# Rebuilding the output projections and MLPs of a two-layer trunk as one stream of matmul groups

## The chip, the cores and the metric

The kernel runs on all 8 cores of one Trainium2 chip, one batch element a core; no core exchanges data with another. A core has TensorE (PE, matmuls), VectorE (DVE), ScalarE (ACT), GpSimd (Pool) and SyncE (SP), and 16 DMA engines, as the page of the profile counts them. The metric is the device time of the slowest core in microseconds, as the median of all executions.

Executions of one kernel fall in two states. In the slow one the four cores of a die (0 to 3 or 4 to 7), or of both, are granted a lower TensorE clock for part of the run. An execution is called slow when one die is over 1% longer than the other at a lower clock, or when it is over 1.5% above the fastest of its kernel. Kernels are compared fast against fast.

## The reference, cut to what matters

```python
# x: (8, 2048, 2048) f32. One mLSTM layer, then one latent-attention layer.
for layer in range(2):
    if layer == 0: mix = mlstm_mixer(x, ...)            # ends in  (sigmoid(o) * hn) @ w_out
    else:          k, v = shared_latent_kv(x, ...);  mix = mla_mixer(x, k, v, ...)   # ends in  o @ w_out
    x = layer_norm(DN_ALPHA * x + mix, ln1_g[layer], ln1_b[layer])
    x = layer_norm(DN_ALPHA * x + square(relu(x @ w1)) @ w2, ln2_g[layer], ln2_b[layer])
```

D is 2048 and D_FF 8192. Each core has 2048 tokens. For a core, one output projection is 1024 matmuls of 128x128 by 128x512, one MLP is 8192.

## The kernel before

It runs its stages one after the other: mLSTM, output projection, MLP, K/V/Q projections, attention, output projection, MLP. A barrier of all engines and all DMAs ends each. A helper records every operation with the buffers that it reads and writes and puts in the semaphore waits; each engine's own operations stand in its program in the order in which they were recorded, and the traces show them in it.

```python
# mLSTM: the convolution weights come with channels on the partitions, four bytes at a time
for j in range(4):
    ld(cw.t[:, :, j], conv_w[j].rearrange("(c p) -> p c", p=128), cw.b[0], allow_slow_non_contiguous=True)
ld(cw.t[:, :, 4], conv_b.rearrange("(c p) -> p c", p=128), cw.b[0], allow_slow_non_contiguous=True)
ld(nwb.t[:], norm_w.partition_broadcast(128), nwb.b[0])
# [...]
def phase_out(C, a_d, aB, fm, W, x_res, xresB, g, b, x_out, xoutB):
    # [... buffers; the whole weight is loaded here, after the barrier ...]
    for nt in range(4):
        P.dma("pool", lambda e, nt=nt: e.dma_start(out=wres[:, :, nt * 512:(nt + 1) * 512],
              in_=W[:, nt * 512:(nt + 1) * 512].rearrange("(k p) n -> p k n", p=128)), writes=[wresB[nt]])
    # [...] prep(tt): load 512 rows of the residual and of a; transpose a on PE
    prep(0)
    for tt in range(S // 512):
        # [...]
        if tt + 1 < S // 512:
            prep(tt + 1)
        stage_tm(...)                        # 16 groups of 16 matmuls, evacuated by DVE
        layernorm_tiles_act(...)             # four norms: three passes on ACT, two on Pool each, and small operations; then x_out to DRAM
    P.barrier()

def phase_mlp2(C, x_in, w1, w2, g, b, x_out, xinB, xoutB):
    # [...]
    build_xT(0)                              # x from DRAM, f32, transposed on PE
    for stile in range(S // 1024):           # two halves of 1024 tokens
        # [... load the eight residual tiles ...]
        for q in range(4):
            # [...] 32 groups h = x @ w1; ACT evacuates with Relu, then Square
            if q == 3 and stile + 1 < S // 1024:
                build_xT(stile + 1)
            # [...] 32 groups xs += h @ w2; DVE evacuates
        layernorm_tiles(C, [xs[:, sub, :] for sub in range(NS)], xsb, gb, bb, gbB, st, store)
    P.barrier()

def layernorm_stats(C, z, zb, stset):        # DVE: 4 bn_stats, 1 bn_aggr; ACT: Ln, Exp; DVE: 1
def layernorm_apply(...):                    # ACT: one pass (scale, bias); DVE: * g, then + b
def layernorm_tiles(...):                    # all eight stats, then all eight apply + store
```

The softmax here doesn't subtract the row's maximum and nothing guards it: scores larger than these inputs give would overflow.

## Time and profile before

| | before |
|---|---|
| recorded first: 6 executions | 7166, 7172, 7191 us (fast), 7402, 7622, 7692 us (slow); median 7296.87 |
| profiled execution (fast), slowest core | 7183.2 us |
| PE busy | 6038.4 us, 84% |
| start to start of two 128x512 matmuls in the MLPs | 0.216 us, clock 1.00 |

From the page: the span, busy time with share of the span and instructions, PE's busy tenths and the granted PE clock in 40 equal slices, and the chain of waits by engine.

```profile
span 7183.2 us, 78102 instructions; the slowest of 8 cores (7125.8 to 7183.2 us)
...
PE 6038.4 (84%) x28080; PEld 2729.0 (38%) x28080; DVE 1675.8 (23%) x2766; ACT 1683.1 (23%) x2829; POOL 811.8 (11%) x1099
...
PE   5899944589999789998488699968499999699995
...
PEclk9999966889999899999799899989799999899997
...
PE 78%; DMA 8%; ACT 4%; POOL 4%; DVE 3%; issue 3%; another core or an unknown queue 1%; SPq 1%; ACTq 0%; DVEq 0%; POOLq 0%
```

PE is nearly always busy inside a stage and falls to 4 tenths at the borders. That is where time can be had: 1145 us of the span are without a matmul. The waits of PE say for what (who, for whom, us in total, times, longest):

```profile
PE p L1290 <- DMA t<-x: 239.7, 18, 84.5
PE p L906 <- DMA t<-hg_d: 206.5, 7, 73.3
PE p L495 <- DMA t<-x: 95.8, 10, 87.0
PE p L427 <- DMA t<-oT_d: 80.0, 2, 61.9
PE p L1312 <- ACT t L1315: 75.8, 2, 38.1
PE p L1312 <- DMA t<-mlp_w: 56.8, 2, 33.0
PE p L671 <- DVE xT_43 L677: 45.9, 3, 43.3
...
PE p L1136 <- DMA t<-v_d: 18.0, 1, 18.0
```

L906 is the transposes of the first output projection, L1290 those of the MLP's x, L427 the projections' matmuls, L1312 the MLP's first matmuls, L1136 attention. The releaser named is the last to come. A wait for x at L1290 is at bottom a wait for the norms before it: x is stored, passes the barrier and is loaded again.

Busy time by stretch (from:to, length, then busy us and instructions of each engine, granted clock, DMA share, GB/s). The rows are the first output projection; the inside of an MLP; the border between the MLP's halves; the first MLP's tail; the last tail.

```profile
902.80:1362.80 460.00, 248.82 (x1281) 123.68 (x1280) 56.14 (x87) 103.94 (x111) 126.20 (x96) 0.76 0.39 106
...
1700.00:2270.00 570.00, 570.00 (x2642) 258.42 (x2641) 48.41 (x70) 116.48 (x190) 22.83 (x20) 1.00 0.50 76
2440.00:2560.00 120.00, 56.23 (x242) 24.59 (x243) 46.12 (x37) 39.54 (x53) 2.28 (x2) 0.72 0.67 175
3378.30:3466.00 87.70, 0.68 (x4) 0.71 (x5) 61.62 (x65) 19.86 (x24) 0.00 (x0) 0.52 0.29 116
...
7102.00:7183.20 81.20, 0.23 (x2) 0.00 (x0) 61.61 (x65) 19.86 (x24) 0.00 (x0) 0.52 0.25 104
```

At the start, the SP queue's own timeline shows the load of the convolution weights (start, length, queue, line, what, count). Its pieces hold the queue from 2.9 to 37 us, and the norm weight behind them comes late. VectorE waits 59 us for that weight, and PE waits 43 us for VectorE. The pieces have 4 bytes, and a load of 8 KB made of them took 24.6 us to land (median of four).

```profile
2.91 26.48 SPq L588 DMA_DIRECT2D cw_105<-a_conv_w  x4
29.43 7.51 SPq L588 DMA_DIRECT2D cw_105<-a_conv_b  x1
36.99 10.10 SPq L588 DMA_DIRECT2D nwb_106<-a_norm_w  x1
```

### The profile page before, as it was taken

How to read it: one execution, taken by the hardware profiler on the slowest of the kernel's cores; microseconds unless marked ns; L12 is line 12 of the kernel's file. 1: busy time of each engine (PE TensorE's matmuls, PEld its weight loads, DVE VectorE, ACT ScalarE, POOL GpSimd, SP SyncE). 2: the span in 40 equal slices, each digit the busy share in tenths (PEclk: the TensorE clock that was granted, in tenths of full speed). 3: DMA queues.
4: the chain of work that ended last, by engine and by line, in shares of the span. 5: the costliest groups of instructions: out<-in, count | busy, mean ns of one | idle time of the engine just before them, and what ended most of it. 6: DMA issues, size and time to landing. Idle time of an engine off the chain costs nothing.

```text
span 7183.2 us, 78102 instructions; the slowest of 8 cores (7125.8 to 7183.2 us)
## 1 busy us (share of the span) xinstructions
PE 6038.4 (84%) x28080; PEld 2729.0 (38%) x28080; DVE 1675.8 (23%) x2766; ACT 1683.1 (23%) x2829; POOL 811.8 (11%) x1099
## 2 busy tenths in 40 slices
PE   5899944589999789998488699968499999699995
PEld 3444422244444334443233222213244444244442
DVE  2566610101110400012332333321100111311004
ACT  2233321221112212210222144432322112211221
POOL 1111122400000000000022400004400000000000
PEclk9999966889999899999799899989799999899997
DMA  6433163275454555452564411135454545545452
GB/s 80 49 44 48 25 148 100 67 161 78 75 78 94 116 97 81 73 80 47 167 109 86 76 60 57 58 91 149 138 139 72 81 73 100 145 71 80 73 81 72
DMA packets 591304, 631.36 MB, mean 88 GB/s; under 512 B 187472, under 2 KB 556496, under 8 KB 566992
## 3 DMA queue, kind: packets, MB, share of 16 engines
q0 software_dynamic: 418320, 332.48, 32.5%
q1 hardware_dynamic: 172608, 293.89, 12.2%
q8 instruction: 233, 3.82, 0.2%
q14 instruction: 143, 1.17, 0.1%
HBM read 845.01 MB, written 113.77 MB: 133 GB/s over the span
## 4 chain that ended last, share of the span: by engine, by line
PE 78%; DMA 8%; ACT 4%; POOL 4%; DVE 3%; issue 3%; another core or an unknown queue 1%; SPq 1%; ACTq 0%; DVEq 0%; POOLq 0%
PE p L1328 25%; PE p L1312 24%; PE p L713 6%; PE p L427 5%; PE p L530 3%; PE p L684 3%; PE p L1147 2%; DMA t<-x 2%; PE p L1138 2%; PE p L1136 2%; PE p L1149 2%; POOL t L361 1%; POOL t L362 1%; DVE t L323 1%; DMA t<-hg_d 1%
## 5 line engine op out<-in xcount | busy, mean ns | idle before, releaser
L1312 PE MATMUL p<-t 128*128 128x512 bf16 x8192 | 1780.4, 380 | 136.1 <-ACT t L1315 75.8
L1328 PE MATMUL p<-t 128*128 128x512 bf16 x8192 | 1770.7, 379 | 0.0
L1312 PEld LDWEIGHTS p<-t 128*128 128x128 bf16 x8192 | 803.4, 98 | 1110.4 <-issue 150.6
L1328 PEld LDWEIGHTS p<-t 128*128 128x128 bf16 x8192 | 801.6, 98 | 966.1
L1315 ACT ACTIVATE t<-p 128x512 f32<-128x512 f32 x512 | 305.6, 597 | 2467.2 <-PE p L1312 2467.2
L1335 DVE TENSOR_TENSOR t<-p,t 128x512 f32<-128x512 f32 x384 | 265.6, 692 | 2163.3 <-PE p L1328 2163.3
L391 POOL DMA_DIRECT2D t<-mlp_w x128 | 146.3, 1143 | 3663.8 <-PE p L1312 1935.7
L427 PE MATMUL p<-t 128*128 128x512 bf16 x2048 | 449.7, 383 | 85.2 <-DMA t<-oT_d 80.0
L1141 ACT ACTIVATE t<-p 128x512 bf16<-128x512 f32 (+3 forms) x640 | 340.2, 533 | 500.8 <-PE p L1138 498.8
L530 PE MATMUL p<-t 128*128 128x512 bf16 x1408 | 325.1, 394 | 79.9 <-DMA t<-b_w_uq 36.3
L1316 ACT ACTIVATE t<-t 128x512 bf16<-128x512 f32 x512 | 322.1, 629 | 48.3 <-ACT t L1315 1.5
L427 PEld LDWEIGHTS p<-t 128*128 128x128 bf16 x2048 | 201.6, 99 | 331.7 <-issue 95.3
L1155 DVE RECIPROCAL t<-p 128x512 f32<-128x512 f32 x64 | 214.9, 3358 | 468.2 <-PE p L1149 459.5
L1290 PE MATMUL p<-ident_sb,t 128*128 128x128 f32 x512 | 93.1, 360 | 241.1 <-DMA t<-x 239.7
L1147 PE MATMUL p<-t 128*128 128x512 bf16 (+3 forms) x640 | 238.1, 372 | 48.8 <-POOL t L1143 38.3
L1332 DVE SCALAR_TENSOR_TENSOR t<-t,p 128x512 f32<-128x512 f32 x128 | 88.0, 688 | 794.2 <-PE p L1328 794.2
L1136 PE MATMUL p<-t 128*128 128x512 bf16 (+3 forms) x640 | 237.0, 370 | 22.6 <-DMA t<-v_d 18.0
L713 PE MATMUL p<-wvo_112,xT_43 128*128 128x512 bf16 x1024 | 233.6, 382 | 22.0 <-DMA wvo_112<-a_w_in 22.0
L530 PEld LDWEIGHTS p<-t 128*128 128x128 bf16 x1408 | 140.0, 101 | 265.3 <-issue 117.0
L1138 PE MATMUL p<-t 64*128 64x512 bf16 (+3 forms) x640 | 238.3, 372 | 0.0
L1149 PE MATMUL p<-t 128*128 128x512 bf16 (+3 forms) x640 | 236.4, 369 | 0.0
L713 PE MATMUL p<-wvo_46,xT_43 128*128 128x512 bf16 x1024 | 231.1, 379 | 0.0
(361 smaller groups left out, 4080.7 us busy)
## 6 DMA issues: line engine op xcount, KB each, us to landing
t<-mlp_w POOLq DMA_DIRECT2D x128, 2048.0 KB, 15.2
t<-x SPq DMA_DIRECT2D x112, 1024.0 KB, 14.4
x<-t SPq DMA_DIRECT2D x48, 1024.0 KB, 3.8
out<-t SPq DMA_DIRECT2D x16, 1024.0 KB, 3.8
wvo_46<-a_w_in POOLq DMA_DIRECT2D x8, 1024.0 KB, 20.4
wvo_112<-a_w_in POOLq DMA_DIRECT2D x8, 1024.0 KB, 18.3
t<-a_w_out POOLq DMA_DIRECT2D x4, 2048.0 KB, 78.5
t<-hg_d SPq DMA_DIRECT2D x16, 512.0 KB, 20.5
```

What stands on the lines that cost most here:

```text
L427: e.matmul(out=pbanks[sub][:], lhsT=lhsT_fn(kc, sub), rhs=rhs_fn(fc), start=first, stop=last),
L530: e.matmul(out=bank[0:m, :], lhsT=wt[:, kc * width + fc * 128: kc * width + fc * 128 + m], rhs=xT[:, kc, tokt * 512:(tokt + 1) * 512], sta ...
L713: P.op("pe", lambda e, kc=kc: e.matmul(out=bk[:], lhsT=xT.t[:, kc, tile * 128:(tile + 1) * 128], rhs=wt[:, kc, :], start=(kc == 0), stop=( ...
L1136: P.op("pe", lambda e, i=i, kt=kt, q0=q0, n=n, ps_=ps_: e.matmul(out=ps_[:, 0:n], lhsT=kn[i][:, kt * 128:(kt + 1) * 128], rhs=qn[i][:, q0: ...
L1138: P.op("pe", lambda e, i=i, kt=kt, q0=q0, n=n, ps_=ps_, r0=r0: e.matmul(out=ps_[:, 0:n], lhsT=kr[r0:r0 + 64, kt * 128:(kt + 1) * 128], rhs ...
L1141: P.op("act", lambda e, pt=pt, ps_=ps_, n=n: e.activation(out=pt[:, 0:n], in_=ps_[:, 0:n], func=AF.Exp, scale=SCALE), reads=[psB], writes= ...
L1147: P.op("pe", lambda e: e.matmul(out=po[:, c0:c0 + n], lhsT=vv[i][:, kt, :], rhs=pt[:, 0:n], start=(kt == 0), stop=(kt == nk - 1)), reads=[ ...
L1149: P.op("pe", lambda e: e.matmul(out=pm[:, c0:c0 + n], lhsT=onesb[:], rhs=pt[:, 0:n], start=(kt == 0), stop=(kt == nk - 1)), reads=[oB, ptB ...
L1312: e.matmul(out=bank[:], lhsT=wt[:, kc * 512 + fc * 128: kc * 512 + (fc + 1) * 128], rhs=xT[:, kc, tk * 512:(tk + 1) * 512], start=(kc == 0 ...
L1315: P.op("act", lambda e, r=r, bank=bank: e.activation(out=r[:], in_=bank[:], func=AF.Relu), reads=[bankB], writes=[rB])
L1316: P.op("act", lambda e, r=r, f=f, tk=tk: e.activation(out=hT[:, f, tk * 512:(tk + 1) * 512], in_=r[:], func=AF.Square), reads=[rB], writes ...
L1328: e.matmul(out=bank[:], lhsT=hT[:, fc, sub * 128:(sub + 1) * 128], rhs=wt[:, fc * 512:(fc + 1) * 512], start=(fc == 0), stop=(fc == 15)),
```

## The change

Intent: keep PE fed across the borders. Work that is not a matmul group is cut in pieces, and each piece is recorded a set number of groups ("slots") after the one that makes its input. Norms leave ACT: statistics and both passes are on DVE, one small power is on Pool. In layer one the projection's weight and first residual and rows are loaded during mLSTM's last head. In layer two the weight is loaded during attention, the rows and the residual after the barrier that ends attention and stays. The first MLP half takes the second 1024 tokens, whose transposed bf16 x the projection leaves on chip; the first 1024 go to DRAM and are read back for the second half. The barriers between mLSTM, projection and MLP go. The convolution weights come as two row loads and a PE transpose; the second v/o weight is loaded a token tile earlier. The input x now comes as f32 over the SP queue and is cast on VectorE and ScalarE (before, Pool's queue loaded it as bf16), and mLSTM's pieces are spaced anew. The core of the diff:

```diff
+class Slots:
+    def later(self, k, fn): # run fn when k more groups have been recorded
+    def slot(self):         # one more group: run what is due
 # mLSTM start
-    for j in range(4):
-        ld(cw.t[:, :, j], conv_w[j].rearrange("(c p) -> p c", p=128), cw.b[0], allow_slow_non_contiguous=True)
+    ld(cwr.t[0:64, :], conv_w.rearrange("j (c p) -> (j c) p", p=128), cwr.b[0])
+    P.op("pe", lambda e: e.transpose(out=pb[3][:, 0:80], in_=cwr.t[:], identity=C.ident[0:80, 0:80]), ...)
 # norms: [...] all of layernorm_stats / _apply / _tiles / _tiles_act goes
+def ln_rstd(C, st, stB):
+    P.op("dve", lambda e: e.bn_aggr(out=st[:, 24:26], in_=st[:, 0:24]), ...)
+    P.op("dve", lambda e: e.tensor_scalar(out=st[:, 26:27], in0=st[:, 25:26], scalar1=LN_EPS, ..., op0=ALU.add), ...)
+    P.op("pool", lambda e: e.tensor_tensor(out=st[:, 27:28], in0=st[:, 26:27], in1=C.mhalf[:], op=ALU.pow), ...)
+def ln_apply(C, st, stB, z, zB, gT, bT):  # two DVE passes of 2048 columns: (z - mean) * g, then * rstd + b
 # output projection [...]
+    def finish(self, sub, gT, bT):
+        ln_rstd(C, st, stB)
+        def apply():
+            ln_apply(C, st, stB, z[:], zB, gT, bT)
+            zb, zbB = self.zb.next()
+            P.op("act", lambda e: e.activation(out=zb[:], in_=z[:], func=AF.Copy), ...)   # bf16
+            # [...] rows 0 to 1023 are also stored
+            def trans():
+                transpose_sub(C, self.tb, zb, zbB, xT.t[:, :, ...], xT.b[0])
+                if sub == 3 or sub == 7:
+                    P.dma("sp", lambda e: e.dma_start(out=self.xT_d[i // 4], in_=xT.t[:]), ...)
+            C.S.later(3, trans)
+        C.S.later(1, apply)
+    def run(self, banks, gT, bT, ring_ready, done=None):
+        for sub in range(14):
+            for nt in range(4):
+                self.group(sub, nt, banks)        # 16 matmuls, DVE evacuates and takes statistics
+                # [...] load(sub + 2), prep(sub + 1)
+                S_.slot()
+            S_.later(1, lambda sub=sub: self.finish(sub, gT, bT))
+        for nt in range(4):
+            for sub in (14, 15):
+                self.group(sub, nt, banks)
+                S_.slot()
+            self.w[nt].free()
+            ring_ready(nt)                        # an MLP panel buffer there; its load one slot later
 # MLP [...]: three panel buffers instead of two, hT in four tiles
+                    w2_group(w, q, nt, sub)
+                    if q == 3 and nt == 3:
+                        S_.later(1, lambda half=half, sub=sub, s=st[sub]: finish(half, sub, *s))
+                S_.later(2, pan.load)
 # whole program
-            phase_mlstm(...)
-            C.P.barrier()
-        phase_out(...)
-        phase_mlp2(...)
+            fin = phase_mlstm(..., freed)          # freed(): loads of the projection as mLSTM's buffers go
+            out_and_mlp(op, 0, banks, gT, bT, fin, x1B, x1TB, x2, x2B)
+            P.barrier()
         phase_kvq(...)
+        for nt in range(4):
+            op.load_w(nt, top=True)                # second weight, under attention
         phase_att(...)
```

## The prediction

> **What bounds it now.** TensorE, except where a stage ends. The page gives PE 84% busy; the chain of waits is 78% PE. In the MLPs 128x512 matmuls start 0.216 us apart at granted clock 1.00 (timeline, stretches), so those stages are at their floor: 8192 matmuls a layer, about 1775 us. [...] What is left is TensorE idle time between stages. From its timeline: start to first projection 72 us, 62 idle; second v/o weight 22; end of mLSTM to first MLP matmul 594, 321 idle; first MLP 1881, 86 idle; norm tail, barrier, reload 87; attention to second MLP's first matmul 443, 189 idle; second MLP 1870, 78 idle; last norm 81.
>
> **What changes.**
> - Start: the convolution weights came by four-byte pieces, which held the SP queue some 35 us and blocked the norm weight, hence VectorE. Now two row loads and a transpose. First projection near 40-45 us, limited by weight transfers: -28 us.
> - Second v/o weight loaded a token tile earlier: -20.
> - First output projection: weights (which landed 41 to 96 us after issue), residual and rows are there before mLSTM ends. Norms no longer form a serial ScalarE/Pool tail (gaps of 73, 70, 84 us); x goes to the MLP through bf16 transposes among matmul groups. Estimate: 1024 x 0.216 + 512 transposes x about 0.07 = 260, with remnants 270. 594 to 270: -324.
> - MLPs: no f32 transposes (L1290, 93 us busy in all), no wait for a half's eight norms (38+33, 38+24 us): 1881 to 1785 and 1870 to 1785: -181.
> - Tails: a norm is about 1.4 us statistics and two passes of 2.3 us (0.692 us per 512 columns, 2.29 per 2048), against 3.5 us of PE per group, so VectorE falls about 25 us behind over the last eight groups. End tail about 32 us, the one before K/V about 40: -96.
> - Second output projection: weights load under attention; after the barrier one row tile and one residual tile: about 15 us instead of 62, then 221 + 23. 443 to 270: -173.
> - Given back: 16 MB of f32 weights compete with attention's first heads: +10.
>
> Unchanged: mLSTM's body (6 us idle in 673), K/V/Q (147 idle), attention (53).
>
> The sum is -812; from 7183 about 6370, all on TensorE's chain. VectorE does about 11 us per 17 us row block in the projections, so does not become the bound.
>
> **Prediction: 6370 us (8 in 10: 6270 to 6520).** The upper side allows for the slow state, which half the executions before show. Faster by over 2%: 0.98; within 2%: 0.015; slower: 0.005.
>
> **What will show it.** PE 92-94% busy. Output projection plus MLP about 2055 us in each layer. No PE gap over 10 us between the mLSTM's last matmul and the first MLP's last. Matmul spacing still 0.216 us. Mean granted clock about 0.97: [...] (0.5 after each long gap). DVE busy time changes little; ACT loses about 250 us.
>
> **What would make it wrong.** [...] buffers handed over late, so that panels or residuals start late; VectorE behind, holding PSUM banks at half boundaries; transfers in the first output projection (about 2.5 MB per 17 us) slower than needed; the first MLP panels landing late.

The floor of 1775 us a layer is the estimate from 8192 matmuls at the 0.216 us of the trace (1769). The clock of 0.5 is read from the clock records of the trace before: in the stretch of the first MLP's tail they show 0.5 from 3381.5 to 3470.2 us, where PE is idle from 3378.3 to 3465.3. The gap from 21 to 65 us, at the start, lies ahead of the first record.

## The result, and the profile after

Ratios are the mean time of one kernel's fast executions over that of the other's in the same rounds, so they are not quite the ratio of the medians.

| | before | after |
|---|---|---|
| all executions, median | 7391.78 us (20) | 6664.97 us (10) |
| range | 7161.89 to 7783.56 | 6401.07 to 7041.99 |
| fast executions | 8 of 20, 7162 to 7246 | 3 of 10: 6401, 6412, 6420 |
| profiled execution (fast) | 7183.2 us | 6396.1 us |
| fast over fast | | 0.8921 (95%: 0.8874 to 0.8969) |

The fast executions lie 30 to 50 us above the forecast of 6370. The recorded median lies 145 us above the upper end of its range, because 7 of the 10 executions were slow. These are two different findings, and the rest keeps them apart.

The same lines of the page after:

```profile
span 6396.1 us, 77157 instructions; the slowest of 8 cores (6334.3 to 6396.1 us)
...
PE 5962.3 (93%) x28081; PEld 2663.5 (42%) x28081; DVE 1874.9 (29%) x2958; ACT 1511.6 (24%) x2589; POOL 524.2 (8%) x937
...
PE   6999999999999999995887599989999999999997
...
PEclk8999999999999999997998799999999999999998
...
PE 84%; DMA 6%; DVE 4%; issue 2%; ACT 2%; POOL 1%; SPq 0%; another core or an unknown queue 0%; ACTq 0%; DVEq 0%; POOLq 0%
```

PE's busy time fell by 76 us, its idle time from 1145 to 434 us (span less busy): nine tenths of the gain is idle time. PE's waits after; L999 is the MLP's first matmuls, L884 the projections, L1284 attention, L426 the K/V/Q stage:

```profile
PE p L1284 <- DMA t<-v_d: 52.0, 1, 52.0
PE p L426 <- DMA t<-x: 48.3, 6, 45.6
...
PE p L999 <- DMA wp_143<-mlp_w: 22.1, 2, 11.8
...
PE p L999 <- DMA wp_184<-mlp_w: 15.8, 2, 9.4
PE p L884 <- DMA aT_165<-oT_d: 15.7, 1, 15.7
...
```

Three of the biggest waits of before (240, 207 and 80 us) have shrunk to one of 16. One has grown: attention's wait for its first head, from 18 to 52 us. Small ones are new, for the MLP's weight panels (wp). By stretch: the whole first projection; the inside of an MLP; after the border of the halves; both tails.

```profile
858.50:1112.60 254.10, 249.90 (x1509) 128.28 (x1510) 165.31 (x219) 85.27 (x77) 16.78 (x24) 1.00 0.51 158
1200.00:2000.00 800.00, 800.00 (x3708) 362.66 (x3707) 104.97 (x153) 133.40 (x218) 33.65 (x30) 1.00 0.52 82
...
2070.00:2130.00 60.00, 48.30 (x211) 21.32 (x212) 0.00 (x0) 16.20 (x27) 2.28 (x2) 0.89 1.01 197
2913.50:2959.20 45.70, 0.06 (x2) 0.06 (x1) 31.14 (x27) 0.00 (x0) 2.74 (x5) 0.54 0.42 169
...
6355.00:6396.00 41.00, 0.00 (x0) 0.00 (x0) 31.04 (x27) 0.00 (x0) 2.74 (x5) 0.53 0.37 154
```

The start, on the SP queue: the convolution weights now take two short issues, and x follows at 4.58 us.

```profile
2.91 0.56 SPq L520 DMA_DIRECT2D cwr_114<-a_conv_w  x1
3.51 0.56 SPq L520 DMA_DIRECT2D cwr_114<-a_conv_b  x1
```

The table below, worked out from the traces, sets the forecast against the result. A stretch runs from a stage's first matmul to the next one's, or to the named end; each entry is the median of the eight cores.

| stretch, us | before | after | change | forecast |
|---|---|---|---|---|
| start to the first q/k group | 71.0 | 44.6 | -26.4 | -28 |
| from there to the first v/o group | 4.9 | 13.7 | +8.8 | 0 |
| rest of mLSTM, to its last v/o group | 812.4 | 795.8 | -16.6 | -20 |
| to the first MLP matmul | 592.7 | 254.1 | -338.6 | -324 |
| first MLP | 1870.9 | 1793.2 | -77.7 | -96 |
| its tail, to the first K/V/Q transpose | 85.8 | 45.6 | -40.2 | -47 |
| K/V/Q, to attention's first matmul | 608.5 | 641.0 | +32.5 | +10 |
| attention | 719.9 | 709.6 | -10.3 | 0 |
| to the second MLP's first matmul | 435.1 | 252.0 | -183.1 | -173 |
| second MLP | 1869.0 | 1781.2 | -87.8 | -85 |
| last tail | 80.9 | 41.1 | -39.8 | -49 |
| sum of the changes | | | -779 | -812 |

### The profile page after: what moved, and what is told of

It reads as the page before. It is cut to its first block, busy times and chain, and to the rows that moved or that the text cites. A ratio compares the mean times of both kernels' runs of the same rounds, so it can differ in the third digit from the quotient of the medians.

```text
span 6396.1 us, 77157 instructions; the slowest of 8 cores (6334.3 to 6396.1 us)
## 1 busy us (share of the span) xinstructions
PE 5962.3 (93%) x28081; PEld 2663.5 (42%) x28081; DVE 1874.9 (29%) x2958; ACT 1511.6 (24%) x2589; POOL 524.2 (8%) x937
## 4 chain that ended last, share of the span: by engine, by line
PE 84%; DMA 6%; DVE 4%; issue 2%; ACT 2%; POOL 1%; SPq 0%; another core or an unknown queue 0%; ACTq 0%; DVEq 0%; POOLq 0%
PE p L1009 27%; PE p L999 26%; PE p L637 7%; PE p L884 7%; PE p L603 4%; PE p L461 3%; PE p L1295 3%; PE p L1286 2%; PE p L1284 2%; PE p L1297 2%; DMA wp_143<-mlp_w 1%; ACT t L1289 1%; DMA wp_184<-mlp_w 1%; PE p L819 1%; PE p L693 1%
## 5 line engine op out<-in xcount | busy, mean ns | idle before, releaser
L461 PE MATMUL p<-t 128*128 128x512 bf16 x1408 | 332.7, 400 | 73.7 <-DMA t<-b_w_uq 34.2
L1002 ACT ACTIVATE rl_149<-p 128x512 f32<-128x512 f32 x128 | 76.4, 597 | 1089.8 <-PE p L999 1089.8
L1002 ACT ACTIVATE rl_190<-p 128x512 f32<-128x512 f32 x128 | 76.4, 597 | 1077.4 <-PE p L999 1077.4
L1284 PE MATMUL p<-t 128*128 128x512 bf16 (+3 forms) x640 | 233.4, 365 | 56.8 <-DMA t<-v_d 52.0
L461 PEld LDWEIGHTS p<-t 128*128 128x128 bf16 x1408 | 141.5, 102 | 265.0 <-issue 130.4
L1016 DVE TENSOR_TENSOR xs_171<-p,xs_171 128x512 f32<-128x512 f32 x24 | 16.6, 691 | 725.0 <-PE p L1009 725.0
L1016 DVE TENSOR_TENSOR xs_126<-p,xs_126 128x512 f32<-128x512 f32 x24 | 16.6, 691 | 725.0 <-PE p L1009 725.0
L999 PE MATMUL p<-xT_109_136,wp_143 128*128 128x512 bf16 x640 | 150.3, 390 | 22.1 <-DMA wp_143<-mlp_w 22.1
L999 PE MATMUL p<-xT_109_136,wp_142 128*128 128x512 bf16 x704 | 161.4, 384 | 4.2 <-DMA wp_142<-mlp_w 4.2
L999 PE MATMUL p<-xT_211_177,wp_184 128*128 128x512 bf16 x640 | 149.3, 388 | 15.8 <-DMA wp_184<-mlp_w 15.8
L1286 PEld LDWEIGHTS p<-t 64*128 64x128 bf16 x640 | 59.7, 93 | 245.6 <-issue 245.6
L999 PE MATMUL p<-xT_211_177,wp_183 128*128 128x512 bf16 x704 | 158.6, 379 | 1.9 <-DVE ost_169 L801 1.9
L999 PE MATMUL p<-xT_109_136,wp_144 128*128 128x512 bf16 x704 | 159.1, 379 | 0.0
L999 PE MATMUL p<-xT_212_178,wp_185 128*128 128x512 bf16 x704 | 159.1, 379 | 0.0
L999 PE MATMUL p<-xT_110_137,wp_144 128*128 128x512 bf16 x704 | 159.1, 379 | 0.0
L999 PE MATMUL p<-xT_211_177,wp_185 128*128 128x512 bf16 x704 | 159.1, 379 | 0.0
L999 PE MATMUL p<-xT_110_137,wp_142 128*128 128x512 bf16 x704 | 158.6, 379 | 0.0
```

The source lines that it names most:

```text
L461: e.matmul(out=bank[0:m, :], lhsT=wt[:, kc * width + fc * 128: kc * width + fc * 128 + m], rhs=xT[:, kc, tokt * 512:(tokt + 1) * 512], sta ...
L999: P.op("pe", lambda e, kc=kc: e.matmul(out=bk[:], lhsT=w.t[:, kc, (f % 4) * 128:(f % 4 + 1) * 128], rhs=xT[tk].t[:, kc, :], start=(kc == 0 ...
L1284: P.op("pe", lambda e, i=i, kt=kt, q0=q0, n=n, ps_=ps_: e.matmul(out=ps_[:, 0:n], lhsT=kn[i][:, kt * 128:(kt + 1) * 128], rhs=qn[i][:, q0: ...
L1286: P.op("pe", lambda e, i=i, kt=kt, q0=q0, n=n, ps_=ps_, r0=r0: e.matmul(out=ps_[:, 0:n], lhsT=kr[r0:r0 + 64, kt * 128:(kt + 1) * 128], rhs ...
```

## The experiments

"Median core" is the median over the eight cores of a core's span in the profiled run (7156.1 before, 6374.0 after, 6378.0 in the repeat `again`). It is steadier than the slowest core. With so few fast executions a time alone seldom settles a few tenths of a per cent. Stretches that an edit doesn't touch vary too: the first MLP took 1792.7 in `again` and 1804.9 in wout_late, attention 712.7 in `again` and 719.6 in late_weights.

### The slow state: again and again2

No edit.

> The changed kernel once more, unchanged, to count states. Fast executions: 6400 to 6420 us, ratio 0.892, under every theory. Theory A (the slow state comes to either kernel alike, and the missed forecast is the missing allowance for it): about half of the executions here and of the kernel before beside it are slow, and a slow execution here costs 150 to 650 us more than a fast one, so that the median of all lies 100 to 300 us over the fast level. Rival B (the denser stream provokes it): at least 25 points more of the executions here are slow than of the kernel before on the same chip. Rival C (the fast forecast itself was off): fast executions outside 6270 to 6520 us.

> The changed kernel unchanged, beside the repaired one on the same chip, and to count states once more. Fast 6395 to 6435 us. Theory A: the share of slow executions is like that of the kernel before (so far 21 of 38) and a slow one costs 150 to 900 us.

`again` gave two fast executions (6398, 6431) and four slow ones (6811 to 7277). `again2` gave one fast (6404) and seven slow (6636 to 7458). Beside them the kernel before had 8 of 11 slow and 7 of 11. All counted executions, by kernel:

| kernel | executions | slow | fast, us | slow, us |
|---|---|---|---|---|
| before | 60 | 35 (58%) | 7162 to 7246 | 7276 to 8133 |
| changed | 24 | 18 (75%) | 6398 to 6431 | 6547 to 7458 |
| the eight kernels derived from it, without zero_mlp | 43 | 27 (63%) | 6342 to 6510 | 6453 to 7431 |
| start_only | 6 | 5 | 7186 | 7467 to 8028 |
| zero_mlp | 8 | 6 | 6408 to 6444 | 6608 to 6770 |

Rival C fell: all the fast executions lie within 6270 to 6520. Theory A held in kind, not in size. In `again` the slow executions cost 397 to 863 us (over the mean of the fast two, 6414), not 150 to 650, and the median of all lay 462 us over them, not 100 to 300. In `again2` the costs were 232 to 1054 us, where 150 to 900 was said. Rival B is not shown and not excluded: on the chip of `again` the changed kernel had fewer slow executions than before (67% against 73%), on that of `again2` more (88% against 64%, 24 points, its bar being 25). Over all, 18 of 24 against 35 of 60 is a difference that chance makes about one time in five (Fisher's test). What is settled is enough for the forecast: when over half of all executions are slow, the median of all is a slow one.

The profile of `again2` fell in the slow state, so one can look inside. Granted clock by die, from its cores view:

```profile
die 0 (median of its cores): 6616.3 us, clock 0.931
die 1 (median of its cores): 6378.5 us, clock 0.968
```

By stretch, columns as above: core 0 (die 0, slow), core 5 (die 1, fast), and core 3 (die 0, slow).

```profile
200.00:860.00 660.00, 660.00 (x2736) 301.75 (x2734) 353.39 (x1000) 169.55 (x403) 93.58 (x220) 0.81 0.31 39
1560.00:2900.00 1340.00, 1317.45 (x6085) 596.04 (x6084) 191.85 (x253) 235.49 (x384) 59.32 (x56) 0.99 0.55 91
```

```profile
200.00:860.00 660.00, 658.38 (x3328) 326.86 (x3326) 427.50 (x1217) 208.55 (x491) 110.50 (x265) 1.00 0.41 59
```

```profile
200.00:860.00 660.00, 658.27 (x3328) 326.76 (x3327) 426.83 (x1216) 208.85 (x491) 109.32 (x262) 1.00 0.44 59
...
5300.00:6500.00 1200.00, 1200.00 (x4571) 497.07 (x4570) 168.06 (x218) 177.93 (x290) 45.52 (x44) 0.81 0.50 81
```

The same code is granted 0.81 on core 0 and 1.00 on core 5. Times count from each core's own start, so this need not be the same moment. And the slow die is not held as one by these times. The clock records give 0.8125 on core 0 in six pieces from 49 us, five us after the start of its first projection group, to 1529 us, 1435 us in all; then full speed to the end. On core 1 the hold is at the same place. On core 3 it lies from 5217 to 6582 us, the end of its matmuls, and on core 2 likewise. Within a hold matmuls start 0.263 us apart, not 0.216. At 0.8125 a TensorE that is always busy would lose 0.1875 of such time, which gives an estimate of 269 us on core 0 and 256 on core 3. They took 256 and 237 us more than the median of die 1. So the size of the loss here is how long a core is held at 0.8125.

What starts and ends a hold is not shown: no run tests it, and the traces do not tell which cores ran at the same moment. In `best`, the other slow profile, all four cores of die 0 lost clock as well (means of 0.871 to 0.876, against 0.968 and 0.969 on die 1). And a short hold can stand in a fast profile: the clock records of the changed kernel give 0.8125 for 74 us in all on core 1, between 3469 and 3628 us, and none on cores 2 to 7.

### zero_mlp

```diff
-                transpose_sub(C, self.tb, zb, zbB, xT.t[...], xT.b[0])
+                transpose_sub(C, self.tb, zb, zbB, xT.t[...], xT.b[0], scale=0.0)   # ACT evacuates times 0
```

> Changed kernel with the x that the two MLPs multiply set to zero (the evacuation of the transposes scales by 0; every instruction and transfer stays; a wrong result on purpose). For the slow state alone; fast executions 6395 to 6435 us under every theory. Theory ([...] the MLPs are over half of the time): slow executions become rarer or cost under half as much as those of the changed kernel beside it, under 350 us. Rival (it has nothing to do with the data): share and cost as in the changed kernel.

The passage cut gave the reason for the theory, which no trace or run shows; what is left to test is whether the data in the matmuls matter.

The result is wrong on purpose. Fast: 6408 and 6444. Slow: 6 of 8, at 6608 to 6770. The share did not fall. The cost did: all six lie under 6771, while in `again2` and `best` on the same chip 9 of the 13 slow executions lie above it, up to 7458. The bound of 350 us was missed by one (6770 is 362 over 6408). Chance alone would put the six so low about one time in 60 (rank test); it is one run of one kernel. Why they cost less is not shown: no slow trace of this kernel was taken, so where its holds lay is not known.

### start_only

```diff
 # the kernel before, with this alone
-    for j in range(4):
-        ld(cw.t[:, :, j], conv_w[j].rearrange("(c p) -> p c", p=128), cw.b[0], allow_slow_non_contiguous=True)
-    ld(cw.t[:, :, 4], ...)
+    ld(cwr.t[0:64, :], conv_w.rearrange("j (c p) -> (j c) p", p=128), cwr.b[0])
+    ld(cwr.t[64:80, :], conv_b.rearrange("(c p) -> c p", p=128), cwr.b[0])
+    # PE transpose into PSUM, one DVE copy to cw
```

> The kernel before, with only the convolution weights loaded as two row blocks and transposed. Theory (the four-byte pieces held the SP queue and, through the norm weight, VectorE): the 43 us wait of the x transposes for VectorE goes, the first projection starts near 45 instead of 72 us, and the time falls by 20 to 28 us (ratio 0.996 to 0.997). Rival (the start is bound by the transfers of the first weights): the first projection may start earlier, but the first v/o group still waits for its weight, and the time falls by at most 12 us (ratio 0.998 or more).

The wait of 43 us is gone, and the first q/k group starts at 37.8 us (median core) instead of 71.0. The first v/o group then waits 12.6 us for its weight and starts at 56.5 instead of 75.9: -19 us there. The one fast execution took 7186 us against 7206 to 7214 beside it. So the theory holds as far as the wait goes, and the rival's limit, the weights, takes the rest. Reaching the first q/k group sooner is not worth its full time: the median core is 7 us under that of the kernel before (7148.7 against 7156.1), so the size of the gain for the whole stays open. The changed kernel reaches this group later than start_only does, at 44.6 us; there PE waits twice, 20.8 us in all, for the cast of x, and the cast for x's transfer.

### late_weights

```diff
             def freed(k):
-                if k < 3:
-                    S_.later(1, lambda: op.load_w(k + 1))
 # after mLSTM's last group
+            for nt in range(4):
+                op.load_w(nt)
```

> Changed kernel, with the four blocks of the first output weight loaded only after the last group of mLSTM is recorded, not during its last head. Theory (their early load is worth the waits of 42 and 17 us that the kernel before shows at this place, somewhat more because the norm pieces now need less time to hide them): TensorE waits 40 to 90 us for them at the first projection's start, the stretch from mLSTM to the first MLP grows from 254 to 310 to 340 us, nothing else moves. Rival (other transfers hide it): under 20 us.

PE waits 47.4 us for the weight, in four pieces, and the stretch to the first MLP goes from 254.1 to 310.8. From the waits of PE:

```profile
PE p L884 <- DMA wo<-a_w_out: 47.4, 4, 24.9
```

The median core took 6451.0 (+77), of which attention, untouched, had 10; the one fast execution 6485.6. The theory held in the stretch (310 to 340 was said). Loading under the last head is worth some 57 of the 339 us gained at this place.

### barriers

```diff
+            S_.drain()
+            P.barrier()
             op.run(banks, gT, bT, ring_ready, done)
+            S_.drain()
+            P.barrier()
```

> Changed kernel, with all pending pieces drained and a barrier of all engines put in before and after each output projection (four in all; early loads stay early). Theory (the gain is TensorE idle time removed at the stage ends, and most of it came from having data there early and from norms off the serial tail, not from the barriers being gone): each barrier costs a drain of 5 to 25 us, the stretch to the first MLP grows from 254 to about 290 us, that to the second from 252 to about 270, total +40 to +70 us. Rival (the missing barriers are the heart of it): +150 us or more.

The stretches to the MLPs are 314.0 and 275.6 (254.1 and 252.0 without); mLSTM's last group comes 10 us later, attention took 8 more. Fast: 6490 and 6510, about 90 us more. That is over the 70 forecast and far under the rival's 150: the first of the two borders costs 60 us, because the barrier exposes both the norm chain (9.9 us for bf16 copies) and the first panel (21.8 us). Of the 522 us gained at these two borders, the missing barriers are worth about 84. (Three of the four stand where the change removed one; the fourth, before the second projection, comes on top of the barrier that ends attention, and the wait there stays at 16 us.)

### via_dram

```diff
-                if sub == 3 or sub == 7:
-                    P.dma("sp", lambda e: e.dma_start(out=self.xT_d[i // 4], in_=xT.t[:]), ...)
+                if sub % 4 == 3:
+                    d, dB = (self.xT_d, self.xTB) if sub < 8 else (self.yT_d, self.yTB)
+                    P.dma("sp", lambda e: e.dma_start(out=d[i // 4], in_=xT.t[:]), reads=xT.b, pw=[dB])
+                if sub == 11 or sub == 15:
+                    xT.b[0].renew()
+                    P.dma("sp", lambda e: e.dma_start(out=xT.t[:], in_=self.yT_d[i // 4]), reads=[self.yTB], pw=xT.b)
```

> Changed kernel, with the second token half's transposed x written to DRAM and read back before the MLP takes it, as the first half is. Theory (the hand-over on chip saves little by itself, because the first eight groups need only the first 512 of these tokens): TensorE waits 10 to 30 us more in each MLP's first 60 us, total +20 to +50 us. Rival (it is the main part of the gain at this border): +80 us or more a layer, the size of the waits of 84 and 80 us for x that the kernel before shows.

PE waits 24.3 us for the read back in two pieces, one a layer, and the MLPs take 1805.5 and 1803.7 (+12 and +22). Fast: 6423 and 6435, ratio 0.8929 against 0.8921 for the change. The median core took 37 us more.

```profile
PE p L1005 <- DMA xT<-yT: 24.3, 2, 14.6
```

So handing the second half over on chip is worth some 17 us a layer by itself. The waits are 9.7 us in the first MLP and 14.6 in the second; the first MLP's +12 alone would be within what this stretch varies. The waits of 84 and 80 us for x did not come back, so skipping DRAM is not what removed them. That x is ready in bf16 and transposed before the MLP needs it is what remains, argued and not tested alone.

### norms_at_end

```diff
-                    if q == 3 and nt == 3:
-                        S_.later(1, lambda half=half, sub=sub, s=st[sub]: finish(half, sub, *s))
                 S_.later(2, pan.load)
+            if q == 3:
+                for sub in range(8):
+                    finish(half, sub, *st[sub])          # finish() applies at once
```

> Changed kernel, with the eight norms of an MLP half recorded together after the half's last matmul group, still on VectorE and Pool, instead of each behind the next groups. Theory (moving the norms off ScalarE took away the 38 us wait at a half's end; taking them in pieces behind later groups only shortens the two tails): no wait over 12 us at the half's end, and the two tails grow by about 15 us each (41 to about 56 us at the end), time +20 to +40 us, ratio about 0.896. Rival (the pieces are what removed the wait): a wait of 30 us or more appears at the end of each first half, time +80 to +120 us, ratio about 0.906.

Neither theory held as it was put. Tails: 62.1 and 57.3, +16 each, as the theory said. But at the border a wait of 32.2 us appeared in the first MLP and one of 23.5 in the second, and the fast executions are at 6476 to 6505, ratio 0.9002: +77 us over `again` on the same chip (median core +103). So the rival was nearer. The wait is not for ACT, though, as it was in the kernel before, but for a weight panel. Pool's timeline shows why:

```profile
2064.09 0.55 POOL L803 TENSOR_TENSOR mst<-mst,mhalf 128x1 f32<-128x1 f32 x1 [5.49 <-DVE mst L802]
2064.76 2.33 POOL L971 DMA_DIRECT2D wp<-mlp_w  x2
```

The panel loads are issued by Pool, behind the eight small powers, which wait for DVE one after the other. The first of them is issued at 2064.76 us, 0.1 us after the last power ends. So the two halves of the question separate: leaving ACT is what removed the 38 us waits for ACT; cutting the norms in pieces is what keeps the panel loads from waiting so long behind them. The second was not seen beforehand.

### apply_late

The changed kernel has a milder form of the same. Its Pool timeline at the border, with the last of eight powers and the two loads behind them (the last matmuls that read this panel buffer end at 2014.6 us):

```profile
2043.54 0.55 POOL L803 TENSOR_TENSOR mst_158<-mst_158,mhalf 128x1 f32<-128x1 f32 x1 [5.49 <-DVE mst_158 L802]
2044.21 1.19 POOL L971 DMA_DIRECT2D wp_143<-mlp_w  x1
2045.39 1.15 POOL L971 DMA_DIRECT2D wp_144<-mlp_w  x1
```

The powers come 6 us apart (the one before started at 2037.51) because each norm's two passes on DVE, 2.3 us each, stand between them. The edit moves those passes back, in the first half alone:

```diff
-        S_.later(1, apply)
+        S_.later(1 if half else 8, apply)
```

> Changed kernel, with the two VectorE passes of the norms at the end of each MLP's first half put off by seven more groups, so that the eight small Pool operations that give the reciprocal deviation are done before the half's last panel load stands in Pool's queue. Theory (that load waits in Pool's queue behind them: it is issued at 2044.2 us, 0.1 us after the last of them ends, 30 us after the matmuls that free its buffer): the loads are issued about 22 us sooner, the waits for the panel (11.8 us in the first MLP, 6.4 in the second) fall under 3 us, the MLPs get 10 and 5 us shorter. Rival (the wait comes from the norms' stores and reloads on the same transfer engines): the issue moves and the wait stays over 8 us.

The load is issued at 2025.3, 19 us sooner, and the next follows 23 us later instead of 1:

```profile
2022.28 3.07 POOL L803 TENSOR_TENSOR mst<-mst,mhalf 128x1 f32<-128x1 f32 x2 [2.55 <-DVE mst L802]
2025.31 1.19 POOL L971 DMA_DIRECT2D wp<-mlp_w  x1
2048.41 1.14 POOL L971 DMA_DIRECT2D wp<-mlp_w  x1 [21.91 <-PE p L999]
```

No wait over 3 us for a panel is left at the border. The MLPs take 1783.4 and 1770.1 (-10 and -11), the fast executions 6384 and 6387, ratio 0.8868. The theory held, and the rival as put, a wait over 8 us with the issue moved, fell. But the transfer has a part. The edit also puts off the stores and reloads, which belong to the pieces moved. The late panel took 37.2 us from issue to landing in the changed kernel, 28.4 here, and 15 to 17 where nothing else moves (the two panels before it); the 1 MB stores of x beside it took up to 21.3 us, the first of them 4.4. PE needed it 25 us after its issue, so at 17 us it would not have waited at all. The wait comes of a late issue and of a slow transfer together; this run does not part them.

### wout_late

```diff
-        for nt in range(4):
-            op.load_w(nt, top=True)
-        ln_load(C, gT, bT, w["ln1_g"][1], w["ln1_b"][1])
+        def head_done(h):                      # called after each head of attention
+            if 2 <= h < 6:
+                op.load_w(h - 2, top=True)
+            if h == 6:
+                ln_load(C, gT, bT, w["ln1_g"][1], w["ln1_b"][1])
```

> Changed kernel, with the 16 MB of the second output weight and its norm vectors loaded after heads 2 to 6 of attention, not at its start. Theory (these loads compete with the first head's loads, the term that was forecast as +10 us): TensorE's wait for v_d at attention's start falls from 52 us to about 18, as in the kernel before; no new wait at the second output projection; fast time about 34 us less, ratio near 0.887. Rival (the longer wait comes from elsewhere, such as the order of the queue after the barrier): the wait stays over 40 us and the time does not move.

The wait at attention's start fell from 52.0 to 18.6 us, and K/V/Q to attention from 641.0 to 614.4:

```profile
PE p L1284 <- DMA t<-v_d: 18.6, 1, 18.6
```

That the load competes with the first head is thus shown, by these 33 us. The time did not follow: median core 6371.3 (-3), one fast execution at 6401. Attention, where the loads now are, took 6 us more (3 more in `again`, with no edit), and the first MLP, recorded ahead of the edit, 12 more. So the forecast of -34 for the whole failed; how much of it is real and how much hidden by the MLP's variation is left open by this run.

### best and repaired

Both are the changed kernel with the edits of wout_late and apply_late and a third: the last three row blocks of a projection, not two, are swept together over the column blocks, so that the first MLP panel's load can start sooner.

```diff
-        for sub in range(14):
+        for sub in range(13):
 # [...]
         for nt in range(4):
-            for sub in (14, 15):
+            for sub in (13, 14, 15):
                 self.group(sub, nt, banks)
```

> Changed kernel with three repairs: the second output weight loaded after heads 2 to 6 of attention; the norms at the end of a first MLP half put off as in apply_late; and the last three row blocks of each output projection swept together over the four column blocks (two before), so that the first block's buffer is free, and the first MLP panel's load can start, about 28 us before the MLP instead of 20. Theory: K/V/Q with attention's start 27 us shorter, MLPs 10 us shorter each, the waits for the first panels (4.2 + 10.3 us, 9.4 us) fall by 8 us a layer; fast executions at 6320 to 6360 us, ratio near 0.880. Rival (the waits only move on to other transfers, as seemed so for the second weight alone): over 6375 us.

`best` gave a wrong result (relative error 0.17). With three norms in a row, block 15's bf16 copy was recorded ahead of the transposes of block 13 and took its buffer. The recorder makes such an order free of races, not right. Its fast executions, 6381 and 6396, show that the rival held, and there are new waits in place of those for the panels. Its profile fell in the slow state; these are the waits of PE on core 5, of the die that was not held:

```profile
PE p L819 <- ACT zb L903: 21.6, 2, 10.8
...
PE p L884 <- ACT aT L825: 12.8, 3, 9.6
```

`repaired` spreads the norms of blocks 13 to 15 and takes the transposes of rows 14 and 15 a group ahead of their use:

```diff
-            C.S.later(3, trans)
+            C.S.later(4 if sub > 12 else 3, trans)
 # [...]
+                if nt == 3:
+                    S_.later(3 if sub == 15 else 1, lambda sub=sub: self.finish(sub, gT, bT))
```

> The kernel called best, whose result was wrong, mended: there the norm of row block 15 was recorded ahead of the transposes of block 13 and overwrote their bf16 copy; now blocks 13 to 15 are spread so that the copies last, and the transposes of rows 14 and 15 stand a group ahead of their use. Theory: a correct result; no wait over 4 us for the first MLP panels, and none over 4 us for the bf16 copies (21.6 us in best on an undisturbed core); the stretches to the MLPs and the MLPs together 30 us shorter than the changed kernel's, K/V/Q 27 us shorter; fast executions 6330 to 6370 us, ratio 0.881 to 0.886. Rival (what is gained is lost to new waits, as in best): over 6380 us, ratio 0.888 or more.

The result is correct. Fast: 6342, 6342 and 6370, ratio 0.8826 (0.8804 to 0.8847). The MLPs take 1773.0 each (-20 and -8); PE's waits list none for a panel or a bf16 copy of over 4 us. K/V/Q took 619.5 (-21, 27 were said), attention 717.0 (+7). With the MLPs and the stretches to them 30 us shorter the theory held. The median core is at 6343.1, 31 us under the changed kernel. It beats both kernels; its median of all six executions is 6495 us, since three were slow.

## Why the prediction was right or wrong

**Wrong: the range.** The step that failed is the sentence "The upper side allows for the slow state, which half the executions before show." The point of 6370 had no term for it at all, and the upper side had 150 us. The measured term is the recorded median less the fast executions' median (6412): 253 us. The data to size it were there: three of the first six executions were slow, by 211 to 501 us over the slowest fast one, 7191, and a median over executions of which more than half are slow lies among the slow ones. With the changed kernel 7 of 10 were slow; its median is the mean of 6551 and 6779, both slow. A range to about 6800 (an estimate: 6370 plus 431, the middle one of the three) or more was called for, or a statement about fast executions alone. The medians of `again` and `again2`, 6876 and 7063, lie above even that.

**Right: the mechanism and the fast time.** 6396 in the profile, 6401 to 6420 in the fast executions, against 6370. That the sum came within 5% is in part luck: the terms that fell short, by 14 to 23 us each (start, MLPs, tails, weight load), were half made up by 35 us of gain beyond the forecast (first projection 15, second 10, attention 10, which was said to be unchanged). The gain is PE idle time at stage borders, and the inside of the stages did not change: 0.216 us from matmul to matmul and clock 1.00 in both.

Point by point, with the table of stretches:

- Start and second v/o weight: -48 said, -34 measured. The first q/k group came as said; the first v/o group after it then waited for its weight (+9; start_only shows the same, more strongly).
- First projection: -324 said, -339 measured. Of this, early weights are worth about 57 (late_weights), the barriers about 60 (barriers), the hand-over on chip next to nothing (via_dram: +2 here, +12 and +22 in the MLPs). These overlap and do not add up. That the rest, over half, is norms off the serial tail and x transposed in time is argued from the trace, not tested alone.
- MLPs: -181 said, -166 measured. The waits for ACT went with the move to DVE (norms_at_end). Waits of 4 to 12 us for panels came, against "No PE gap over 10 us": two of 10.3 and 11.8. The one of 11.8, at the half border, comes of Pool's order, which the prediction did not name, and of its slow transfer, 37.2 us against 15 to 17 (apply_late). The one of 10.3, at the MLP's start, is a first panel landing late, as it warned.
- Tails: -96 said, -80 measured. DVE's lag was forecast at 25 us and the tail at 32; it is 41. Cut in pieces is still what makes them short: they grow by 16 each without (norms_at_end).
- Second projection: -173 said, -183 measured; the wait after the barrier is 15.7 us (15 said).
- Given back: +10 said, +32 measured in K/V/Q, of which 27 go when wout_late moves the weight's load. Mis-sized threefold.
- Signs: PE 93% (92 to 94 said); projection and MLP 2047 and 2033 us (2055 said); clock 0.968 as said (median core). DVE was said to change little: it gained 199 us, as the projection's norms came to it from ACT and Pool. ACT lost 172, not 250.
- The idle window: for each gap of PE over 20 us but the first the clock records show 0.5, to between 3 and 11 us past its end (3381.5 to 3470.2 us for the gap from 3378.3 to 3465.3 before, 2917.0 to 2964.8 for that from 2913.5 to 2959.2 after); with the gaps gone these records fell from 1148 us (core 5 before) to 430 (core 1 after), and the mean clock rose from 0.92 to 0.97.

## What to carry to other kernels

Look at the executions' states before you forecast a median: if more than half of them fall in a slow state, the median is a slow execution, and its allowance is a term of the sum like any other. When stages end in serial tails, forecast by adding up TensorE's idle time stretch by stretch; it held within 5% here, with some luck. When you cut work in pieces behind other work, look at each engine's queue for what now stands behind a piece that waits: here small powers of 0.55 us on Pool held up the issue of a weight load by 30 us, and one number in the recording order mended it.
